# A decoder layer's final norm, moved from a closing pass over token blocks to lists of rows by expert group, worked on between the experts' steps

## Chip, core and metric

The kernel runs on one core of one Trainium2 chip. The core has five engines with a queue of instructions each: TensorE (PE in the rows, with its weight loads as PEld), VectorE (DVE), ScalarE (ACT), GpSimd (POOL), and SyncE (SP), which here only starts transfers. The metric is the device time of one execution in microseconds, lower is better.

## What is computed

The layer mixes 1024 tokens of width 1024 by two attention branches, adds the residual, and applies a first layer norm. Then comes a mixture of experts: each token picks one of 4 groups, and two of the 8 experts in that group. A second residual and layer norm give the output. The part that matters:

```python
grp = jnp.argmax(lg, axis=-1)                       # one group of 4 for each token
top_v, top_i = lax.top_k(lf, MOE_TOP_K)             # two experts of that group's 8
expert = grp[:, None] * EXP_PER_GROUP + top_i       # 0..31
...
    return (jax.nn.silu(g) * u) @ w_down[e]         # one expert on its tokens
...
h = layer_norm(ALPHA * h + ffn, ln2_g[l], ln2_b[l]) # over 1024 columns of each token
```

With the inputs of `setup_inputs()` the groups get 223, 248, 278 and 275 tokens, no expert gets more than 107, and 167 tokens of the last group use neither expert 30 nor expert 31.

## The kernel before

The program has three stages: projections and attention; the output projection with first norm and routing; and the experts, from about 1050 us to the end. The change is in the last.

**Experts.** The outer loop (L1676) goes over `seq`, 32 experts with 12 steps each. At a step PE multiplies one 128x1024 slab of weights with 128 gathered token rows: steps 0 to 7 are the gate and up weights, steps 8 to 11 the down weights. Everything is done in float32 split in two fp32r parts, so before a slab can be used ACT rounds it (`eh`, L1479) and DVE subtracts the rounded part from the raw slab (`el`, L1480). A step has six matmuls, four with `eh`, two with `el` (L1497). There are three `eh` buffers. `ahead` (L1657) emits the ACT and DVE work two to three steps ahead of the matmuls.

After step 7 comes a chain between engines: silu on ACT (L1504), product on DVE (`act`, L1505), transposes on PE (L1514), a rounding on ACT and a difference on DVE (`at`, L1516 and L1517). Then steps 8 to 11 run. `put` (L1519) scales the result on ACT (`y`) and adds its rows to `ybuf` in memory by an indirect transfer from POOL (L1523). `gather_rows` (L1372), also on POOL, fetches the rows of the expert after next from `hbuf`.

The order on PE, DVE, ACT and POOL is the order of the program text from here on (`manual_schedule`, L1668): each engine takes its instructions one after the other. SP's queue holds the weight loads (L1528). They go to a ring of 41 slots (`ring`, L1437) of 128x1024, and a load waits until the slot's last user is done.

**Final norm.** `ybuf` starts as the residual, and every expert adds into it. At (28,2), (28,4), (29,2) and (29,4) the marks `K` in `TAIL` (L65) spread the norm's gain and bias over partitions: two float32 matmuls (L1569) and a copy (L1570) each, in `final_gb`. After expert 30, `final_load` reads all eight blocks of 128 tokens. After the last step of expert 31 the long text in `TAIL` runs: `final_stats` and `final_stats_act` (L1577, L1583) take mean and variance of a block on DVE or ACT, `root` and `newton` (L1201, L1206) the inverse root, and gain and bias are applied on DVE, ACT and POOL (L1598 to L1613). Rows of expert 31 get its result from PSUM in `last_add` (L1625), are normed by `finish_rows` (L1540), and are written last by `put_rows` (L1549).

After that a hardware loop (L1713) makes extra passes for experts with over 128 tokens; its count `ntot` is 0 with these inputs.

Of the kernel before, what the change touches and what calls it, by code (L numbers as in the profile page):

```python
# [63 lines left out]
GBL = (22, 0)  # L64
TAIL = {(30, 11): "L0 L1 L2 L3 L4 L5 L6 L7", (28, 2): "K", (28, 4): "K", (29, 2): "K", (29, 4): "K", (31, 9): "P", (31, 11): "S0 V01 S1 N01 U0 A3 S2 V13 D2 G0p A5 S4 N13 V35 R D4 U1 B0p N35 G1p E2 H4 D5 B1p A7 Z A6 V58 U3 G3p D7 N58 E5 U6 G6p E7 B3d C6p F X"}  # L65
# [11 lines left out]
def tile_hybrid(ctx: ExitStack, tc: tile.TileContext, x, xT, w_t, w_gate, pos_k, w1_k, w2_k, pos_v, w1_v, w2_v,  # L77
# [1085 lines left out]
    nof, tok8 = (rc_pool.tile([128, NB], FP, name=n) for n in ("nof", "tok8"))  # L1163
    nid = rc_pool.tile([128, NB], I32, name="nid")
    nc.gpsimd.iota(tok8, pattern=[[128, NB]], base=0, channel_multiplier=1, allow_small_or_imprecise_dtypes=True)
# [120 lines left out]
    def out_route(b, L):  # L1286
# [8 lines left out]
        nc.vector.tensor_scalar(e4, e4, sc_[:, 1:2], None, op0=OP.is_equal)  # L1295
        nc.vector.tensor_scalar(e4, e4, -1.0, 1.0e30, op0=OP.add, op1=OP.mult)
# [21 lines left out]
        nc.vector.tensor_tensor(nof[:, b:b + 1], oh[:, 0, NE - 1:NE], oh[:, 1, NE - 1:NE], op=OP.add)  # L1318
# [94 lines left out]

    nc.vector.scalar_tensor_tensor(nid, nof, 4096.0, tok8, op0=OP.mult, op1=OP.add)
# [12 lines left out]
    nc.vector.tensor_copy(ntot, CX[:, 31:32])  # L1427
# [112 lines left out]
    def finish_rows(pl, z, o, g2, b2):  # L1540

        def centre(mean):
            nc.vector.scalar_tensor_tensor(o, z, mean, g2, op0=OP.subtract, op1=OP.mult)
        r, _, _ = stats(pl, z, EPS / ALPHA ** 2, centre, ((0, 512), (512, 1024)))
        for i in range(2):
            c = slice(i * 512, i * 512 + 512)
            nc.vector.scalar_tensor_tensor(o[:, c], o[:, c], r, b2[:, c], op0=OP.mult, op1=OP.add)
# [8 lines left out]
    zs = {}  # L1556

    def final_gb():

        kept.extend([next(er_at) for _ in range(3)])  # L1560
        gb, *ts = (p(n) for p, n in zip(kept, ("gb", "g2", "b2")))
        for i, src in enumerate((ln2_g, ln2_b)):
            nc.sync.dma_start(gb[32 * i:32 * i + 1, :], bass.AP(tensor=src.tensor, offset=src.offset,
                                                              ap=[[0, 1], [1, 1024]]))
        yield
        for i, t in enumerate(ts):
            for h in range(2):
                c, ps = slice(h * 512, h * 512 + 512), bank("pt")
                nc.tensor.matmul(ps, ones[32 * i:32 * i + 1, :], gb[32 * i:32 * i + 1, c], start=True, stop=True)  # L1569
                nc.scalar.copy(t[:, c], ps)  # L1570
                yield ts

    def final_load(b):
        zs[b] = er("zf")
        nc.sync.dma_start(zs[b], ybuf[b * 128:b * 128 + 128, :])

    def final_stats(b):  # L1577
        bs = fmt[:, b, 2:14].rearrange("p (a b) -> p a b", a=2)
        for i in range(2):
            nc.vector.bn_stats(bs[:, i], zs[b][:, i * 512:i * 512 + 512])  # L1580
        nc.vector.bn_aggr(fmt[:, b, 0:2], fmt[:, b, 2:14])

    def final_stats_act(b):  # L1583

        os_[b] = er("of")
        mean, var, s1 = fmt[:, b, 0:1], fmt[:, b, 1:2], fmt[:, b, 2:3]
        nc.scalar.activation(os_[b], zs[b], AF.Copy, scale=1.0 / D, accum_out=mean)
        nc.scalar.activation(os_[b], zs[b], AF.Square, scale=-1.0, bias=mean, accum_out=s1)
        nc.scalar.activation(var, s1, AF.Copy, scale=1.0 / D)

    def final_root(a, n):
        root(fmt[:, a:n], *(fmv[:, i, a:n] for i in range(3)), EPS / ALPHA ** 2)

    def final_newton(a, n):
        newton(fmt[:, a:n], *(fmv[:, i, a:n] for i in range(4)))

    def final_unit(b):
        nc.scalar.activation(zs[b], zs[b], AF.Identity, scale=fmv[:, 1, b:b + 1], bias=fmv[:, 3, b:b + 1])  # L1598

    def final_shift(b):  # L1600
        nc.vector.scalar_tensor_tensor(zs[b], zs[b], fmt[:, b, 0:1], gb[0], op0=OP.subtract, op1=OP.mult)

    def final_scale(b, skip=False):
        o = os_[b] if b in os_ else er("of")
        nc.vector.scalar_tensor_tensor(o, zs[b], fmv[:, 1, b:b + 1], gb[1], op0=OP.mult, op1=OP.add)
        final_put(b, o, skip)

    def final_gain(b, eng):
        eng.tensor_tensor(zs[b], zs[b], gb[0], op=OP.mult)

    def final_bias(b, eng, skip=False):
        o = os_[b] if b in os_ else er("of")
        eng.tensor_tensor(o, zs[b], gb[1], op=OP.add)  # L1613
        final_put(b, o, skip)

    def final_put(b, o, skip):
        if skip:
            outs.append(put_rows(o, nid[:, b:b + 1], outs + fulls))
        else:
            fulls.append(nc.sync.dma_start(out[0, b * 128:b * 128 + 128, :], o))  # L1620

    os_, outs, fulls, gb, hold = {}, [], [], [], [HOLD]
    fmt, fmv = e_pool.tile([128, NB, 14], FP, name="fmt"), e_pool.tile([128, 4, NB], FP, name="fmv")

    def last_add():  # L1625
        for i in range(2):
            c = slice(i * 512, i * 512 + 512)
            nc.vector.scalar_tensor_tensor(zl[:, c], last.dn[i], last.wgt, zg[:, c], op0=OP.mult, op1=OP.add)

    def final(text):  # L1630
        eng = {"p": nc.gpsimd, "d": nc.vector}
        f = {"L": final_load, "S": final_stats, "A": final_stats_act, "U": final_unit, "V": final_root, "N": final_newton,
             "D": final_shift, "E": final_scale, "H": lambda b: final_scale(b, True)}
        for t in text.split():
            if t[0] in "GBC":
                (final_gain if t[0] == "G" else final_bias)(int(t[1]), eng[t[2]], *[True][:t[0] == "C"])
            elif t == "W":
                hold[0] = 0
            elif t == "P":
                nc.scalar.preload_act_table_set(LNEXP)  # L1640
            elif t == "Z":
                last_add()
            elif t == "F":
                finish_rows(e_pool, zl, ol, *gb)
            elif t == "K":
                gb[:] = next(gb_)
            elif t == "R":
                rows_of(zg, last.ids)
            elif t == "X":
                outs.append(put_rows(ol, last.ids, outs))  # L1650
            else:
                f[t[0]](*map(int, t[1:]))
# [23 lines left out]
    for i, (e, k) in enumerate(seq):  # L1676
# [18 lines left out]
        if (e, k) in TAIL:  # L1695


            final(TAIL[e, k])
# [131 lines left out]
```

## Time and profile before

| | |
|---|---|
| median of 3 runs | 1719.45 us (1716.68 to 1721.52) |
| the profiled execution's own time | 1719.97 us |
| its span in the trace | 1718.2 us |
| busy, whole span: PE / DVE / ACT / POOL | 1587.5 / 1264.3 / 1103.8 / 439.2 us |
| transfers | 308.85 MB, mean 180 GB/s |

The span runs from the first instruction to the last event of the profiled execution; its own time is 1.8 us more. Times in rows are microseconds from the span's start unless marked ns. In a timeline row, "x7" merges seven instructions of one kind that ran without a pause, and a bracket tells how long the engine had been idle and whose end released it.

### The profile page before, as it was taken

The page shows a single profiled execution, that of the slowest core. Times are in us where ns is not written, and L with a number is a line of the kernel's source. Part 1 is how long each engine was busy: PE and PEld are TensorE (multiplying, and loading weights), DVE is VectorE, ACT ScalarE, POOL GpSimd, SP SyncE. Part 2 cuts the span into 40 slices and gives each one's busy share as a digit, 9 for nine tenths or more (in the row PEclk, how much of TensorE's full clock was granted, in tenths as well). Part 3 has the DMA queues.
Part 4 walks back from the last instruction along what each step waited for, and adds up shares of the span by engine and source line. Part 5 has one row for each costly group of instructions (what it writes and reads, how often), then busy time and mean ns, then how long its engine had stood idle before and what let it go on. Part 6 is the DMA issues. An engine that isn't in the chain of part 4 may idle for free. (4 is left out here: it accounts for less than half of the span.)

```text
span 1718.2 us, 24639 instructions
## 1 busy us (share of the span) xinstructions
PE 1587.5 (92%) x8114; PEld 1310.5 (76%) x8114; DVE 1264.3 (74%) x2680; ACT 1103.8 (64%) x2037; POOL 439.2 (26%) x390
## 2 busy tenths in 40 slices
PE   7999999998899999999799996999999999999970
PEld 6888888777678988788678895777777777777750
DVE  5555553347867774588877797998998899889786
ACT  4566665525557785578933014887887888788772
POOL 1011122341223332323610242221121212113134
PEclk9999999999999999999999997999999999999995
DMA  4111112232320111001356769999999999999532
GB/s 172 38 37 38 37 38 68 74 101 89 123 86 35 36 47 33 25 18 57 96 177 212 292 213 346 353 364 358 362 366 354 367 359 329 370 364 370 164 118 102
DMA packets 104518, 308.85 MB, mean 180 GB/s; under 512 B 20387, under 2 KB 24611, under 8 KB 104388
## 3 DMA queue, kind: packets, MB, share of 16 engines
q1 hardware_dynamic: 94228, 289.25, 46.0%
q0 software_dynamic: 10160, 18.00, 4.2%
q8 instruction: 65, 1.06, 0.3%
q14 instruction: 65, 0.53, 0.1%
HBM read 283.18 MB, written 41.17 MB: 189 GB/s over the span
## 5 line engine op out<-in xcount | busy, mean ns | idle before, releaser
L1480 DVE TENSOR_TENSOR el<-er,eh 128x1024 fp32r<-128x1024 f32 x384 | 448.1, 1219 | 31.7 <-ACT eh L1479 29.8
L1479 ACT CAST eh<-er 128x1024 fp32r<-128x1024 f32 x384 | 391.0, 1056 | 43.8 <-PE pt L1497 29.1
L232 PE MATMUL pp<-xh,wh 128*128 128x512 f32 x672 | 273.7, 407 | 1.6 <-DVE q L287 1.6
L234 PE MATMUL pp<-xh,wl 128*128 128x512 f32 x672 | 265.9, 396 | 0.0
L233 PE MATMUL pp<-xl,wh 128*128 128x512 f32 x672 | 264.4, 393 | 0.0
L1497 PE MATMUL av<-eh,xt 128*128 128x512 f32 x512 | 196.9, 395 | 1.4 <-ACT xt L1466 1.2
L1497 PE MATMUL pt<-eh,xt 128*128 128x512 f32 x512 | 196.2, 393 | 0.0
L1523 POOL DMA_INDIRECT ybuf<-y,idx x30 | 95.9, 3198 | 212.3 <-ACT y L1522 205.6
L234 PEld LDWEIGHTS pp<-xh,wl 128*128 128x128 f32 x672 | 127.1, 189 | 29.7
L232 PEld LDWEIGHTS pp<-xh,wh 128*128 128x128 f32 x672 | 127.5, 190 | 21.1 <-DVE q L287 2.0
L233 PEld LDWEIGHTS pp<-xl,wh 128*128 128x128 f32 x672 | 127.7, 190 | 19.4
L1497 PE MATMUL sc<-eh,at 128*128 128x512 f32 x512 | 141.4, 398 | 0.0
L892 POOL TENSOR_TENSOR pw<-pw,st 128x64 f32<-128x64 f32 (+5 forms) x128 | 85.9, 701 | 183.2 <-DVE st L887 156.5
L1497 PEld LDWEIGHTS av<-eh,xt 128*128 128x128 f32 x512 | 96.4, 188 | 27.8 <-ACT eh L1479 3.0
L1497 PEld LDWEIGHTS pt<-eh,xt 128*128 128x128 f32 x512 | 96.5, 189 | 22.2
L930 DVE TENSOR_TENSOR PT<-pt,PT 128x512 fp32r<-128x512 f32 (+1 forms) x136 | 90.9, 671 | 25.1 <-ACT PT L929 23.6
L1497 PEld LDWEIGHTS sc<-eh,at 128*128 128x128 f32 x512 | 93.6, 188 | 20.1 <-ACT eh L1479 0.4
L1497 PE MATMUL av<-el,xt 128*128 128x512 f32 x256 | 104.6, 409 | 0.0
L1497 PE MATMUL pt<-el,xt 128*128 128x512 f32 x256 | 100.9, 394 | 0.0
L1372 POOL DMA_INDIRECT xg<-hbuf,idx x31 | 33.3, 1075 | 253.3 <-PE pp L1460 239.6
L123 POOL TENSOR_TENSOR wl<-wr,wh 128x1024 fp32r<-128x1024 f32 x24 | 59.0, 2458 | 140.1 <-ACT wh L122 120.5
L929 ACT CAST PT<-pt 128x512 fp32r<-128x512 f32 (+1 forms) x136 | 76.7, 567 | 16.7 <-PE pt L922 15.0
(431 smaller groups left out, 3586.0 us busy)
## 6 DMA issues: line engine op xcount, KB each, us to landing
er<-in_w_gu_dram SPq DMA_DIRECT2D x256, 512.0 KB, 7.7
er<-in_w_dn_dram SPq DMA_DIRECT2D x128, 512.0 KB, 7.2
wr<-in_w_t_dram SPq DMA_DIRECT2D x44, 512.0 KB, 3.3
mgd<-mg SPq DMA_DIRECT2D x32, 256.0 KB, 2.0
G<-mgd SPq DMA_DIRECT2D x32, 256.0 KB, 3.4
xr<-in_xT_dram SPq DMA_DIRECT2D x8, 512.0 KB, 8.7
wo<-in_w_oT_dram SPq DMA_DIRECT2D x8, 512.0 KB, 4.8
wor<-in_w_out_dram SPq DMA_DIRECT2D x8, 512.0 KB, 7.6
```

Source lines behind the costliest of these rows:

```text
L123: (eng or nc.vector).tensor_tensor(lo, raw, hi.bitcast(FP), op=OP.subtract)
L232: nc.tensor.matmul(ps, wh[:, kk], xh[k][:, c], start=k == 0, stop=False)
L233: nc.tensor.matmul(ps, wh[:, kk], xl[k][:, c], start=False, stop=False)
L234: nc.tensor.matmul(ps, wl[:, kk], xh[k][:, c], start=False, stop=k == 7)
L892: nc.gpsimd.tensor_tensor(t, t, st[:, 1, hi_, i:i + 1].to_broadcast([128, w]), op=OP.mult)
L929: nc.scalar.copy(t[:, 0], src)
L930: nc.vector.tensor_tensor(t[:, 1], src, t[:, 0].bitcast(FP), op=OP.subtract)
L1372: nc.gpsimd.indirect_dma_start(out=t, out_offset=None, in_=hbuf, in_offset=bass.IndirectOffsetOnAxis(ap=ids, axis=0), bounds_check=S - 1, ...
L1479: nc.scalar.copy(wh, r)
L1480: nc.vector.tensor_tensor(wl, r, wh.bitcast(FP), op=OP.subtract)
L1497: nc.tensor.matmul(pss[h], a[j == 1][:, kk], (wl if j == 2 else wh)[:, h], start=o == 0 and j == 0, stop=o == n - 1 and j == 2)
L1523: nc.gpsimd.indirect_dma_start(out=ybuf, out_offset=bass.IndirectOffsetOnAxis(ap=self.ids, axis=0), in_=y, in_offset=None, bounds_check=S ...
```

## The change

- While the second expert runs, a generator `lists` builds a table of token numbers sorted by group. Tokens that use expert 30 or 31 are left out of the last group's list. This takes 31 small DVE instructions, three small matmuls, eight indirect transfers from POOL to a table `tabf` in memory, and one load of it on SP. Gain and bias are loaded already spread over partitions; the four `K` marks are gone.
- `FIN` names eleven blocks of up to 128 rows of a list and the step (expert, k) where each begins: nine between experts 10 and 28, two in expert 31. A twelfth block holds expert 30's rows, a thirteenth expert 31's.
- A block's work is spread over steps by `at(i, f)`, run at the end of step i: `take` (an indirect gather of `ybuf` rows on POOL, four steps ahead), `fin_mean` and `fin_square` on ACT in the next two steps, `turn` in the third (two integer instructions on DVE give a first guess of the inverse root, three rounds of four 128x1 instructions on POOL refine it, and DVE subtracts the mean and multiplies by the gain), and `end` in the fifth (DVE multiplies by the root and adds the bias, POOL scatters the rows to the output). Rows go in place, in a slot `zf` of the ring; `fm` is a 128x8 tile of statistics, `any` a scratch output.
- Expert 30's block adds that expert's result from PSUM at (30,11) and is normed during expert 31. Expert 31's block is normed after the last matmul, as before, but with nothing ahead of it.
- The extra passes' count is raised to 32 if a list overflows its blocks (`NFB`).

```diff
-GBL = (22, 0)
-TAIL = {(30, 11): "L0 L1 L2 L3 L4 L5 L6 L7", (28, 2): "K", (28, 4): "K", (29, 2): "K", (29, 4): "K", (31, 9): "P", (31, 11): "S0 V01 S1 N01 U0 A3 S2 V13 D2 G0p A5 S4 N13 V35 R D4 U1 B0p N35 G1p E2 H4 D5 B1p A7 Z A6 V58 U3 G3p D7 N58 E5 U6 G6p E7 B3d C6p F X"}
+NFB = 3, 3, 3, 2
+FIN = {(10, 0): (0, 0), (12, 0): (0, 1), (14, 0): (0, 2), (18, 0): (1, 0), (20, 0): (1, 1), (22, 0): (1, 2),
+       (25, 0): (2, 0), (26, 0): (2, 1), (28, 0): (2, 2), (31, 0): (3, 0), (31, 1): (3, 1)}
...
+    def lists():
+        kept.extend([next(er_at) for _ in range(3)])
+        gb[:] = (p(n) for p, n in zip(kept, ("g2", "b2", "any")))
+        for t, src in zip(gb, (ln2_g, ln2_b)):
+            nc.sync.dma_start(t, bass.AP(tensor=src.tensor, offset=src.offset, ap=[[0, 128], [1, 1024]]))
...
+        for b in range(NB):
+            s_ = nc.gpsimd.indirect_dma_start(out=tabf, out_offset=bass.IndirectOffsetOnAxis(ap=at[:, b:b + 1], axis=0),
+                                              in_=nid[:, b, :], in_offset=None, bounds_check=128 * 32 - 1,
+                                              oob_is_err=False)
...
+    def fin_mean(z, f):
+        nc.scalar.activation(gb[2], z, AF.Copy, scale=1.0 / D, accum_out=f[:, 0:1])
+
+    def fin_square(z, f):
+        nc.scalar.activation(gb[2], z, AF.Square, scale=-1.0, bias=f[:, 0:1], accum_out=f[:, 1:2])
+        nc.vector.tensor_scalar(f[:, 2:3], f[:, 1:2], VE, None, op0=OP.add)
+
+    def fin_root(f, act=False):
...
+            b = t.bitcast(I32)
+            nc.vector.tensor_scalar(b, v.bitcast(I32), 1, None, op0=OP.logical_shift_right)
+            nc.vector.tensor_scalar(r.bitcast(I32), b, -1.0, float(0x5f3759df), op0=OP.mult, op1=OP.add)
+            for _ in range(3):
+                nc.gpsimd.tensor_tensor(t, r, r, op=OP.mult)
+                nc.gpsimd.tensor_tensor(t, t, v, op=OP.mult)
+                nc.gpsimd.tensor_scalar(t, t, -0.5, 1.5, op0=OP.mult, op1=OP.add)
+                nc.gpsimd.tensor_tensor(r, r, t, op=OP.mult)
...
+    def fin_shift(o, z, f):
+        nc.vector.scalar_tensor_tensor(o, z, f[:, 0:1], gb[0], op0=OP.subtract, op1=OP.mult)
+
+    def fin_scale(o, f, cut=1):
...
+            nc.vector.scalar_tensor_tensor(o[:, c], o[:, c], f[:, 3:4], gb[1][:, c], op0=OP.mult, op1=OP.add)
...
+    def block(i, ids, x=None):
+
+        b = {}
+
+        def take():
+            b["z"], b["f"] = er("zf"), fin_new()
+            rows_of(b["z"], ids)
+
+        def add():
             for h in range(2):
+                add_rows(b["z"], b["z"], x, h)
+
+        def turn():
+            for _ in fin_root(b["f"]):
+                pass
+            fin_shift(b["z"], b["z"], b["f"])
+
+        def end():
+            fin_scale(b["z"], b["f"])
+            s_ = put_rows(b["z"], ids, outs)
...
+        at(i - 4 if x is None else i - 3, take)
+        if x:
+            at(i, add)
+            i += 4
+        at(i + 1, lambda: fin_mean(b["z"], b["f"]))
+        at(i + 2, lambda: fin_square(b["z"], b["f"]))
+        at(i + 3, turn)
+        at(i + 5, end)
...
+    block(12 * NE - 13, idx[:, NE - 2, 0:1], ex[NE - 2])
+    for (e, k), (c, i) in FIN.items():
+        block(12 * e + k, idf[:, 8 * c + i, 0:1])
...
+        zl, ol = er("zl"), er("ol")
+        finish_rows(ol, zl, last, zg)
+        put_rows(ol, last.ids, outs)
+    at(12 * NE - 5, lambda: rows_of(zg, last.ids))
+    at(12 * NE - 4, lambda: nc.scalar.preload_act_table_set(LNEXP))
+    at(12 * NE - 1, final)
```

How the queues change at three places (each row is an instruction in an engine's order, "x8" eight alike; line numbers of the changed kernel are one higher here for the same line).

DVE, steps 0 to 7 of an expert, before:

```order
L1467 TENSOR_TENSOR xt<-pp,xt 128x512
L1480 TENSOR_TENSOR el<-er,eh 128x1024
L1467 TENSOR_TENSOR xt<-pp,xt 128x512
L1480 TENSOR_TENSOR el<-er,eh 128x1024 x8
L1505 TENSOR_TENSOR act<-act,av 128x256
L1505 TENSOR_TENSOR act<-act,pt 128x256
```

and in expert 10 of the changed kernel, the first with a block:

```order
L1468 TENSOR_TENSOR xt<-pp,xt 128x512
L1481 TENSOR_TENSOR el<-er,eh 128x1024 x5
L1625 TENSOR_SCALAR fm<-fm 128x1
L1481 TENSOR_TENSOR el<-er,eh 128x1024
L1639 TENSOR_SCALAR fm<-fm 128x1
L1640 TENSOR_SCALAR fm<-fm 128x1
L1650 SCALAR_TENSOR_TENSOR zf<-zf,fm,g_11025 128x1024
L1481 TENSOR_TENSOR el<-er,eh 128x1024 x2
L1655 SCALAR_TENSOR_TENSOR zf<-zf,fm,b_11026 128x1024
L1506 TENSOR_TENSOR act<-act,av 128x256
L1506 TENSOR_TENSOR act<-act,pt 128x256
```

Five instructions of the block now stand among the eight `el` of the steps, the last of them straight ahead of the silu chain's `act`.

ACT at the same place, before:

```order
L1479 CAST eh<-er 128x1024 x2
L1521 ACTIVATE y<-sc,idx 128x512
L1522 ACTIVATE y<-sc,idx 128x512
L1479 CAST eh<-er 128x1024 x6
L1504 ACTIVATE act<-av 128x256
```

and in expert 10 of the changed kernel:

```order
L1522 ACTIVATE y<-sc,idx 128x512
L1523 ACTIVATE y<-sc,idx 128x512
L1480 CAST eh<-er 128x1024 x2
L1621 ACTIVATE any,fm<-zf 128x1024
L1480 CAST eh<-er 128x1024
L1624 ACTIVATE any,fm<-zf,fm 128x1024
L1480 CAST eh<-er 128x1024 x3
L1505 ACTIVATE act<-av 128x256
```

The two passes over the block stand between the casts for steps 4 and 5, and 5 and 6.

POOL at the end of the program (`xg` is the buffer into which expert 31's rows of `ybuf` are gathered for the final add), before:

```order
L1372 DMA xg_9419<-hbuf,idx 128x1024
L1523 DMA ybuf<-y,idx 1024x1024 x2
L1609 TENSOR_TENSOR zf<-zf,g_15003 128x1024
L1536 DMA xg_9419<-ybuf,idx 128x1024
L1613 TENSOR_TENSOR of<-zf,b_15004 128x1024
```

and in the changed kernel, the end of the third and last root refinement in expert 31 and what follows:

```order
L1642 TENSOR_TENSOR fm<-fm 128x1
L1643 TENSOR_TENSOR fm<-fm 128x1
L1644 TENSOR_SCALAR fm<-fm 128x1
L1645 TENSOR_TENSOR fm<-fm 128x1
L1607 DMA out_dram<-zf,idf 1024x1024
L1537 DMA xg_9421<-ybuf,idx 128x1024
L1607 DMA out_dram<-zf,idx 1024x1024
L1607 DMA out_dram<-ol,idx 1024x1024
```

The gather for the last add now stands behind 36 refinement instructions and two scatters of the blocks in expert 31.

## Rows read from the trace of the kernel before

**Rows 1.** Busy time in one stretch of the experts: PE, PEld, DVE, ACT, POOL, clock, DMA share, GB/s.

```profile
1200.00:1300.00 100.00, 98.47 (x450) 77.30 (x449) 88.14 (x97) 82.42 (x109) 18.47 (x11) 1.00 0.99 364
```

**Rows 2.** Who waited for whom, 1100 to 1600 us: total us, times, longest us.

```profile
PEld av L1497 <- DVE el L1480: 9.3, 26, 0.4
...
ACT eh L1479 <- DMA er<-in_w_gu_dram: 5.6, 17, 0.3
```

**Rows 3.** The same for SP's queue, 960 to 1640 us.

```profile
SPq L1528 <- PE pt L1497: 219.7, 229, 3.1
```

**Rows 4.** Timeline of one expert, ACT and DVE, steps 1 to 7 and the chain's start.

```profile
1321.25 8.05 DVE L1480 TENSOR_TENSOR el<-er,eh 128x1024 fp32r<-128x1024 f32 x7
...
1325.61 1.05 ACT L1479 CAST eh<-er 128x1024 fp32r<-128x1024 f32 x1 [0.34 <-PE pt L1497]
...
1331.36 0.42 DVE L1505 TENSOR_TENSOR act<-act,av 128x256 f32<-128x256 f32 x1 [0.67 <-ACT act L1504]
```

**Rows 5.** POOL's timeline: scatters of two neighbouring experts, then of experts 27 and 28.

```profile
1303.77 2.45 POOL L1523 DMA_INDIRECT ybuf<-y,idx  x1 [6.75 <-ACT y L1522]
1322.62 2.44 POOL L1523 DMA_INDIRECT ybuf<-y,idx  x1 [6.76 <-ACT y L1522]
...
1586.17 2.44 POOL L1523 DMA_INDIRECT ybuf<-y,idx  x1 [6.75 <-ACT y L1522]
1607.52 2.44 POOL L1523 DMA_INDIRECT ybuf<-y,idx  x1 [6.76 <-ACT y L1522]
```

**Rows 6.** Timeline of the end: last matmuls, last add, last block's statistics, last scatter.

```profile
core 0 of [0], span 1718.2 us
...
1663.47 0.62 PE L1497 MATMUL sc<-el,at 128*128 128x512 f32 x2
...
1683.56 1.39 DVE L1628 SCALAR_TENSOR_TENSOR zl<-sc,idx,xg 128x512 f32<-128x512 f32 x2
...
1698.58 1.27 DVE L1190 BATCH_NORM_STATS2 bs<-zl 128x6 f32<-128x512 f32 x2
...
1703.65 0.98 POOL L1550 DMA_INDIRECT out_dram<-ol,idx  x1 [4.14 <-DVEq L1713]
```

**Rows 7.** Timeline of the end: instructions of the kinds that a block is made of.

```profile
1668.26 1.04 ACT L1587 ACTIVATE of<-zf 128x1024 f32<-128x1024 f32 x1
...
1669.42 1.15 ACT L1588 ACTIVATE of<-zf,fmt 128x1024 f32<-128x1024 f32 x1
...
...
1670.72 1.27 DVE L1601 SCALAR_TENSOR_TENSOR zf<-zf,fmt,g 128x1024 f32<-128x1024 f32 x1
...
1677.10 0.16 DVE L1208 TENSOR_TENSOR fmv<-fmv 128x2 f32<-128x2 f32 x1
1677.30 0.16 DVE L1209 SCALAR_TENSOR_TENSOR fmv<-fmv 128x2 f32<-128x2 f32 x1
```

**Rows 8.** Timeline of the end: POOL and DVE arithmetic at the same time.

```profile
1672.97 2.34 POOL L1613 TENSOR_TENSOR of<-zf,b 128x1024 f32<-128x1024 f32 x1
1673.35 1.98 DVE L1208 TENSOR_TENSOR fmv<-fmv 128x2 f32<-128x2 f32 x1
...
1688.63 5.65 POOL L1609 TENSOR_TENSOR zf<-zf,g 128x1024 f32<-128x1024 f32 x2 [1.72 <-ACT zf L1598]
1688.71 6.65 DVE L1605 SCALAR_TENSOR_TENSOR of<-zf,fmv,b 128x1024 f32<-128x1024 f32 x2
```

**Rows 9.** POOL's instructions by shape: busy us, mean ns of one, idle us before them.

```profile
L892 POOL TENSOR_TENSOR pw<-pw,st 128x640 f32<-128x640 f32 x32 | 41.3, 1292 | 0.0
...
L892 POOL TENSOR_TENSOR pw<-pw,st 128x64 f32<-128x64 f32 x64 | 25.4, 396 | 183.2 <-DVE st L887 156.5 <-ACT PT L929 17.9 <-PE sc L371 7.8
...
L892 POOL TENSOR_TENSOR pw<-pw,st 128x128 f32<-128x128 f32 x8 | 3.2, 401 | 0.0
```

**Rows 10.** Transfers, from issue to landing (last figure, us), and POOL issuing a scatter.

```profile
xg<-ybuf,idx POOLq DMA_INDIRECT x1, 5.1
...
1682.71 1.83 POOL L1550 DMA_INDIRECT out_dram<-of,nid  x1 [2.69 <-DVE of L1605]
```

More of the change, by code (lines that the diff above doesn't have):

```diff
@@ L1538, in rows_of @@
                                      bounds_check=S - 1, oob_is_err=False)
[L1540 to L1547, printed above, removed]
+    outs, gb = [], []
@@ L1573, in final_load @@
[L1573 to L1606, printed above, removed]
@@ L1623, in tile_hybrid @@
[L1623 to L1652, printed above, removed]
@@ new lines, in fin_shift, with finish_rows @@
+    def fin_shift(o, z, f):
+        nc.vector.scalar_tensor_tensor(o, z, f[:, 0:1], gb[0], op0=OP.subtract, op1=OP.mult)
+    def fin_scale(o, f, cut=1):
+        for i in range(cut):
+            c = slice(i * 1024 // cut, (i + 1) * 1024 // cut)
+            nc.vector.scalar_tensor_tensor(o[:, c], o[:, c], f[:, 3:4], gb[1][:, c], op0=OP.mult, op1=OP.add)
+    def finish_rows(o, z, x=None, g=None):
+        f = fin_new()
+        bs = e_pool.tile([128, 2, 6], FP, name="bs", tag="bs", bufs=2)
+        mt = e_pool.tile([128, 2], FP, name="mt", tag="mt", bufs=2)
+        for i in range(2):
+            if x:
+                add_rows(z, g, x, i)
+            nc.vector.bn_stats(bs[:, i], z[:, i * 512:i * 512 + 512])
+        nc.vector.bn_aggr(mt, bs.rearrange("p a b -> p (a b)"))
+        nc.vector.tensor_scalar(f[:, 2:3], mt[:, 1:2], float(D), VE, op0=OP.mult, op1=OP.add)
+        r = fin_root(f, x is not None)
+        next(r)
+        fin_shift(o, z, mt)
+        next(r)
+        fin_scale(o, f, 2)
@@ new lines, in tile_hybrid, with final @@
+    steps_ = lists()
+    for i in (13, 16, 17, 18, 19):
+        at(i, lambda: next(steps_, None))
+    block(12 * NE - 13, idx[:, NE - 2, 0:1], ex[NE - 2])
+    for (e, k), (c, i) in FIN.items():
+        block(12 * e + k, idf[:, 8 * c + i, 0:1])
+    last, zl = ex[NE - 1], None
+    def final():
+        nonlocal zl
+        zl, ol = er("zl"), er("ol")
[3 more added lines that the diff above has]
+    at(12 * NE - 4, lambda: nc.scalar.preload_act_table_set(LNEXP))
@@ L1691, in tile_hybrid @@
             ex[e].put()
-        if (e, k) == GBL:
-            gb_ = final_gb()
-            next(gb_)
-        if (e, k) in TAIL:
-            final(TAIL[e, k])
-        if (e, k) == (NE - 2, 11):
-            zl, ol = er("zl"), er("ol")
+        for f in hooks.pop(i, ()):
+            f()
+    assert not hooks
     mo_.close()
```

134 lines of the change are left out of this document (96 added, 38 removed).

## Prediction

> **What bounds the kernel now.** I read the windows first, to see which engine fills the experts' stage. In 100 us of it PE is busy 98.5, DVE 88.1 and ACT 82.4 us, and POOL 18.5 [rows 1]. So PE sets the pace, at 18.85 us an expert, the distance of two scatters [rows 5], and DVE is left 11.9% of that, 2.2 us.
>
> Then the waits: does PE ever wait, and for whom? It does, 26 times in 500 us and always about 0.35 us, for DVE's difference `el` [rows 2]. That is once per expert for that kind of wait, so DVE has no lead over PE at that point. The transfers are no limit: ACT waited 5.6 us in all for weights [rows 2], while SP waited 219.7 us for PE to free a slot [rows 3], so the loads run as far ahead as the ring lets them.
>
> Then the timeline of one expert, for where DVE and ACT have their idle time. DVE runs seven `el` in 8.05 us without a pause, 1.15 us each. ACT pauses 0.34 us, for PE, before the cast of step 6. DVE's one larger pause is 0.67 us, at the head of the silu chain [rows 4]. What is put on DVE before that point delays the chain, with 0.67 us to absorb it.
>
> Last, the end. The last matmuls end at 1663.47 + 0.62 = 1664.1 us, the span at 1718.2 [rows 6]: 54.1 us with PE idle.
>
> **What the change removes.** After the last matmul there remain two adds (1.4 us, as the row of 1683.56), what now lies between the last block's statistics and its scatter (1703.65 - 1698.58 = 5.1), and what lies from there to the end (1718.2 - 1703.65 = 14.5) [rows 6]: 21.0 us where there were 54.1. **Saved: 33.1 us.** The `K` marks made expert 28 take 1607.52 - 1586.17 = 21.35 us in place of 18.85 [rows 5], and expert 29 has two as well. **Saved: 2 x 2.5 = 5.0 us.** The eight reads of `ybuf` and six of the eight writes of the output leave SP's queue after the last weight load, where nothing waits behind them.
>
> **What a block costs.** I take expert 10, with the queues as the two places on DVE and ACT show them.
> 1. *ACT.* The mean takes 1.16 us from its start to the next start, the square, by its 1.15 and the same 0.12 for reading the sum, 1.27 [rows 7]. Both stand before the cast of step 6, which had 0.34 us to spare, so it comes 2.1 us late. DVE ran some 0.3 us behind that cast (the sixth `el` of the merged row starts at 1321.25 + 5 x 1.15 = 1327.0, the cast ends at 1326.7 [rows 4]), so its `el` of step 6 is 1.8 us late.
> 2. *DVE's own work.* The instruction on the variance falls into that wait. Two small ones are 0.2 us each from start to start, shift and scale 1.27 us each [rows 7]: 2.9 us.
> 3. *The refinement on POOL.* Twelve dependent 128x1 instructions, and the scale on DVE waits for the last. No row has this shape. From 128x640 to 128x128 the time falls by 1.74 ns a column, which leaves 0.18 us at one column; 128x64 took 0.40 [rows 9]. I take 0.20, as nearer the line, and 0.05 between two: 3.0 us if POOL is left alone.
> It is not: a 128x2 instruction that is 0.16 us elsewhere [rows 7] took 1.98 us on DVE beside one on POOL, and ended when that did [rows 8]. And two POOL and two DVE instructions took turns, POOL's pair 5.65 us where 2 x 2.34 is its own, DVE's 6.65 where 2.5 is [rows 8]. So each waits while the other runs. Between the guess and the scale DVE has three long instructions (shift, `el` of steps 7 and 8). Each lets one refinement step through at its end: three steps, 0.6 us more for DVE. The other nine, 9 x 0.25 = 2.25, run while DVE waits at the scale. Together 2.85 us.
> 4. *Absorbed:* the 0.67 us ahead of the chain.
>
> Behind the waiting scale stands `act`, for which PE's transposes and steps 8 to 11 wait, so all of it reaches PE: 1.8 + 2.9 + 2.85 - 0.7 = 6.9 us. **Nine blocks: 62 us.**
>
> Whether that [rows 8] also holds for `el` against such tiny instructions, no row shows. The Trainium skill's page "SBUF — State Buffer", section "Who interferes with whom", says that a DVE instruction with two SBUF inputs contends with a GpSimd instruction that reads SBUF, and that whichever starts first holds the shared ports for its whole length. `el`, shift and scale are of that kind, so by the page point 3 costs what I took; without it, nothing.
>
> **Expert 31** has three blocks. The first costs 6.9 us. The second's refinement queues on POOL behind the first's: between the two scales DVE has two small instructions (0.4), the third block's shift (1.27), the lock (0.6), nine refinement steps (2.25) and the second scale (1.27), 5.8 us. The two adds of expert 30's result take 1.4. Sum 14 us. The third refinement comes after, beside steps 8 to 11. But the gather for the last add stands behind it, as the POOL place shows: after the second scale POOL issues a scatter (1.83 us), runs twelve steps (3.0, plus three waits of 1.2 for `el`), issues the next scatter (1.83), then the gather, which lands 5.1 us after issue [rows 10]: 15.3 us. PE needs some 8.7 from there to its end (an estimate: four steps at 18.85 / 12, and 2.4 for the chain). So the add waits some 6 us. **20 us.**
>
> **The lists.** 31 small dependent DVE instructions at 0.2 us, less the 0.67: **5.5 us.** The three matmuls and one ACT pass lie beside them. Eight indirect transfers hold POOL some 10 us in expert 1; the next gather is needed 18.85 us later. SP waits for the table before one weight load; the ring of 41 slots, which the loads keep filled [rows 3], covers that with some three experts' steps. If it didn't, PE would wait a few us once.
>
> **Sum:** -33.1 - 5.0 + 5.5 + 62 + 20 = +49.4. Against the profiled execution's own 1719.97 us that is 1769.4; that execution is 0.5 us above the median, so **1769 us**. With a refinement step of 0.40 + 0.05 us, point 3 is 5.25, nine blocks cost 22 us more and expert 31 some 6: 1797, the upper end.
>
> **Rivals.**
> - *No lock for small steps.* The refinement runs beside DVE's 3.5 us of shift and two `el`, and costs nothing. A block is 1.8 + 2.9 - 0.7 = 4.0 us. Nine are 36, expert 31 is 4.0 + 2.9 + 1.4 and 3 for the gather, 11. Sum -38.1 + 5.5 + 47 = +14: 1734 us. For it: no row shows so short an instruction on POOL. Against it: the short one on DVE waited [rows 8].
> - *The idle time takes the blocks* (the other side). DVE's 2.2 us an expert absorb most of a block's 3.1 us (three small instructions, shift, scale), ACT's 17.6% all of its 2.4, and refinement hides. Then 0.9 us a block, 8 for nine, 4 for expert 31: -38.1 + 5.5 + 12 = -21, 1699 us. It decides where a block costs under some 2.8 us: (38.1 - 5.5 - 7) / 9. Against it: most of that idle time lies inside the silu chain, after the block's last instruction, and 0.67 is left before it [rows 4].
> - *Memory is the limit.* The transfers' share is 0.99 at 364 GB/s [rows 1]. Then DVE's and ACT's work would hide, and the rows' way through memory, 4.2 MB read and 4.2 written, would cost 8.4 MB / 364 GB/s = 23 us: -38.1 + 23 = -15, 1704 us. Against it: SP waits for PE, not PE for loads [rows 2, 3]. The Trainium skill's page "SBUF — State Buffer", section "SBUF: two separate sides", puts HBM to one core at about 358 GB/s and calls HBM almost always the bottleneck; the trace's rate agrees, its waits don't.
> - *The change doesn't do what it says:* a list overflows and 32 extra passes run. The group sizes (223, 248, 278 of 384; 167 of 256) exclude it.
>
> **How the numbers follow.** About 0.3% (5 us) is what a measurement can tell from no change. The forecast, lock and late gather, has 0.62. The rival without lock has 0.23, the idle time 0.07, memory 0.02. A block of just under 3 us, so no change, has 0.04, and over the upper end is 0.02. Faster is 0.07 + 0.02 = 0.09, same 0.04, slower 0.87. The range runs from 1730, which takes in the rival without lock, to 1797; it leaves out 0.15. The forecast's own range is 1750 to 1797.
>
> **What would show it.** Expert 10 takes about 25.7 us between scatters and expert 11 18.85. On DVE the scale of expert 10 stands behind an idle stretch of 2 us or more that POOL's refinement ended, and POOL's first steps last over 1 us, the later ones 0.2. ACT's cast of step 6 no longer waits for PE. In expert 31 the add on DVE waits for a transfer. From the first add to the end it is 21 us. An expert with a block at under 21.6 us would prove me wrong on the sign; one at 22.8, with the scale not waiting, on the lock.

## The result and the profile after

| | before | changed |
|---|---|---|
| median | 1719.76 us (1716.68 to 1721.52, 4 runs) | 1766.64 us (1762.49 to 1769.04, 4 runs) |
| ratio, 95% interval | 1 | 1.0272 (1.0244 to 1.030) |
| span of the profiled execution | 1718.2 us | 1767.2 us |
| mean granted clock | 0.972 | 0.963 |

The kernel became 2.7% slower, 47 us. 1769 was forecast.

The rows that answer to those shown of before, first the busy time in a stretch with one block, in expert 10 (columns as in [rows 1]):

```profile
1200.00:1300.00 100.00, 93.81 (x412) 73.09 (x411) 84.32 (x94) 77.12 (x102) 27.04 (x24) 0.97 0.95 344
```

PE is busy 93.8 of 100 us in place of 98.5, and POOL's 27.0 is no sign of a limit. Who waited for whom, 1100 to 1640 us (total, times, longest):

```profile
PEld av L1515 <- DVE act L1506: 31.1, 8, 3.9
...
PEld av L1498 <- DVE el L1481: 24.1, 35, 1.8
DVE zf L1655 <- POOL fm L1645: 20.3, 8, 2.5
```

The first and the third are new: PE's transposes wait for `act`, and DVE's scale waits for POOL's refinement, 2.5 us a block. This is the wait that the forecast put at the head of the silu chain. The second was 9.3 us in 26 waits of 0.4 at most [rows 2]; now single ones are 1.8.

I measure experts by PE's first transpose of the chain (L1515), since the scatters of [rows 5] shift by some 3 us where they wait for a block's gather. PE's rows for experts 9, 10 (with a block) and 11:

```profile
1244.15 0.41 PE L1515 MATMUL av<-ident,act 128*128 128x128 f32 x2
...
1269.21 0.69 PE L1515 MATMUL av<-ident,act 128*128 128x128 f32 x2 [3.66 <-DVE act L1506]
...
1289.88 0.40 PE L1515 MATMUL av<-ident,act 128*128 128x128 f32 x2
```

Expert 10 takes 25.06 us and expert 11 takes 20.67, where an expert without a block takes 18.82 by the same mark. So the block costs 6.24 us up to its chain and 1.85 more behind it. Over the 20 intervals from expert 9 to expert 29 it is 1683.69 - 1244.15 = 439.54 us, less 20 x 18.82 = 376.4: **63.1 us for nine blocks**, 55.3 of them ahead of the chains and 7.8 in the experts behind. The blocks are not alike: up to the chain experts 14 and 22 cost 5.62 and 5.63 us, expert 10 costs 6.24, and expert 26, which follows a block directly, 7.25.

Now the timeline of DVE in expert 10, from the `el` of step 5 to the chain, then POOL's:

```profile
1257.98 1.23 DVE L1481 TENSOR_TENSOR el<-er,eh 128x1024 fp32r<-128x1024 f32 x1 [0.98 <-ACT eh L1480]
...
1260.06 1.22 DVE L1481 TENSOR_TENSOR el<-er,eh 128x1024 fp32r<-128x1024 f32 x1 [0.78 <-ACT eh L1480]
1261.20 0.15 DVE L1639 TENSOR_SCALAR fm<-fm 128x1 int32<-128x1 int32 x1
1261.38 0.15 DVE L1640 TENSOR_SCALAR fm<-fm 128x1 int32<-128x1 int32 x1
1261.45 1.27 DVE L1650 SCALAR_TENSOR_TENSOR zf<-zf,fm,g 128x1024 f32<-128x1024 f32 x1
1262.64 2.35 DVE L1481 TENSOR_TENSOR el<-er,eh 128x1024 fp32r<-128x1024 f32 x2
1267.54 1.28 DVE L1655 SCALAR_TENSOR_TENSOR zf<-zf,fm,b 128x1024 f32<-128x1024 f32 x1 [2.54 <-POOL fm L1645]
1268.74 0.41 DVE L1506 TENSOR_TENSOR act<-act,av 128x256 f32<-128x256 f32 x1
```

```profile
1261.63 1.15 POOL L1642 TENSOR_TENSOR fm<-fm 128x1 f32<-128x1 f32 x1 [3.14 <-DVE fm L1640]
1262.86 1.05 POOL L1643 TENSOR_TENSOR fm<-fm 128x1 f32<-128x1 f32 x1
1264.00 1.04 POOL L1644 TENSOR_SCALAR fm<-fm 128x1 f32<-128x1 f32 x1
1265.13 0.19 POOL L1645 TENSOR_TENSOR fm<-fm 128x1 f32<-128x1 f32 x1
...
1267.31 0.19 POOL L1645 TENSOR_TENSOR fm<-fm 128x1 f32<-128x1 f32 x1
```

All parts of the price stand here in one column of starts. DVE waits 0.98 + 0.78 = 1.76 us for casts that ACT does late. Not all of that is the price of ACT's two passes, since in expert 10 the mean itself waits for its rows. In expert 14 it doesn't, the first of the two waits is 0.37 us, and the sum is 1.15. ACT's row of expert 10, then DVE's of expert 14:

```profile
1255.86 1.06 ACT L1621 ACTIVATE any<-zf 128x1024 f32<-128x1024 f32 x1 [0.50 <-DMA zf<-ybuf,idf]
...
1348.15 1.23 DVE L1481 TENSOR_TENSOR el<-er,eh 128x1024 fp32r<-128x1024 f32 x1 [0.37 <-ACT eh L1480]
```

Guess, shift and scale take 0.25 + 1.19 + 1.20 = 2.64, with the variance instruction 2.8. Three refinement steps last over a microsecond, each ending just after one of DVE's three long instructions; the nine others take 0.19 with 0.08 between, and DVE stands 2.54 us until they are done. `act` comes last, with PE behind it.

And the end: PE's last matmuls, the add, its gather and the last scatter.

```profile
1742.27 0.63 PE L1498 MATMUL sc<-el,at 128*128 128x512 f32 x2
```

```profile
1747.33 0.75 DVE L1676 SCALAR_TENSOR_TENSOR zl<-sc,idx,xg 128x512 f32<-128x512 f32 x1 [5.49 <-DMA xg<-ybuf,idx]
```

```profile
1743.04 1.04 POOL L1537 DMA_INDIRECT xg<-ybuf,idx  x1 [0.30 <-PEq L1784]
...
1754.00 0.97 POOL L1607 DMA_INDIRECT out_dram<-ol,idx  x1 [8.61 <-DVEq L1784]
```

From the first add to the end it is 1767.2 - 1747.3 = 19.9 us, and the add waited 5.5 us for a gather that POOL issued at 1743.04, after PE had ended. Before, from the last add to the end it was 34.6 us [rows 6].

What I had not looked for is the clock. Busy time and clock in three pieces around expert 10's chain:

```profile
1262.00:1268.00 6.00, 2.17 (x11) 1.27 (x9) 3.46 (x4) 0.77 (x2) 4.59 (x12) 1.00 0.95 332
1268.20:1274.80 6.60, 5.59 (x17) 4.69 (x18) 5.22 (x8) 4.17 (x6) 2.14 (x2) 0.50 0.51 190
1275.00:1281.00 6.00, 6.00 (x28) 4.86 (x27) 4.92 (x6) 5.40 (x7) 0.43 (x1) 1.00 0.85 277
```

PE had work for 2.2 of 6 us, and then the granted clock is 0.50 for 6.6 us, the level of 1.2 GHz, just when steps 8 to 11 run. Four matmuls take 2.05 us there and 1.08 at full clock:

```profile
1270.83 2.05 PE L1498 MATMUL sc<-eh,at 128*128 128x512 f32 x4
...
1275.58 1.08 PE L1498 MATMUL sc<-eh,at 128*128 128x512 f32 x4
```

Each of the nine blocks has such a stretch, of 3.4 or 6.8 us; before, the experts had none, up to the end of PE's work. This is the time behind the chains: 1.85 us in expert 11, behind a stretch of 6.8 us, and 0.73 to 1.00 in the seven experts behind a stretch of 3.4.

### The profile page after: what moved, and what is told of

Read it like the earlier page. It is cut to its first block, busy times and chain, and to the rows that moved or that the text cites. A ratio compares the mean times of both kernels' runs of the same rounds, so it can differ in the third digit from the quotient of the medians.

```text
span 1767.2 us, 24910 instructions
## 1 busy us (share of the span) xinstructions
PE 1608.2 (91%) x8109; PEld 1326.8 (75%) x8109; DVE 1270.3 (72%) x2730; ACT 1111.4 (63%) x2050; POOL 489.5 (28%) x562
## 5 line engine op out<-in xcount | busy, mean ns | idle before, releaser
L1498 PE MATMUL sc<-eh,at 128*128 128x512 f32 x512 | 154.2, 426 | 0.0
L1524 POOL DMA_INDIRECT ybuf<-y,idx x30 | 68.9, 2295 | 206.1 <-ACT y L1523 145.9
L1498 PEld LDWEIGHTS sc<-eh,at 128*128 128x128 f32 x512 | 102.6, 206 | 22.8 <-ACT at L1517 0.4
```

The source lines that it names most:

```text
L1498: nc.tensor.matmul(pss[h], a[j == 1][:, kk], (wl if j == 2 else wh)[:, h], start=o == 0 and j == 0, stop=o == n - 1 and j == 2)
L1524: nc.gpsimd.indirect_dma_start(out=ybuf, out_offset=bass.IndirectOffsetOnAxis(ap=self.ids, axis=0), in_=y, in_offset=None, bounds_check=S ...
```

## The experiments

All times are medians beside runs of the kernel before on the same chip; "after" is the changed kernel. The price of the nine blocks is taken from each trace as above, from the last expert ahead of them to the last one behind, less 18.82 an expert; it leaves out the time before the experts, by which the traces differ by up to 8.5 us (expert 0's transposes start between 1062.2 and 1070.7).

**Scale moved behind the chain.**

```diff
-        at(i + 5, end)
+        at(i + (8 if i < 12 * NE - 12 else 5), end)
```

> Of the nine blocks in experts 10 to 28, only the scale (and its scatter) moves, from the end of step 5 to the end of step 8, behind the silu chain; POOL's twelve refinement steps stay. Theory (the price is the time DVE stands at the scale with act behind it): the chain is late by ACT's 1.76 us, the guess 0.25 and the shift 1.19, less 0.67, so 2.5 us, and the scale costs 0 to 1.2 us more behind the chain. Nine blocks cost 22 to 33 us in place of 63: 1726 to 1737 us, 8 more if the clock still falls after each block. POOL's steps last about 1.1 us beside el and 0.19 us where DVE pauses, and el stays at 1.15 us. Rival (a POOL step delays DVE as much as DVE delays it): twelve steps beside el and the chain cost DVE some 0.2 us each, 2.4 us a block, and the gain is given back: 1750 to 1758 us, with el pairs longer than 2.35 us.

Measured: 1757.0 us, ratio 1.0229 (1.0186 to 1.0271). The time is that of the rival, the trace is not: a pair of `el` still takes 2.35 us with POOL's steps beside it, and expert 10 costs 21.05 + 20.02 - 37.64 = 3.4 us, as the theory has it. But the nine cost 53 us, because another wait, 2.1 us in all in the changed kernel, has grown:

```profile
ACT any L1621 <- DMA zf<-ybuf,idf: 21.5, 8, 5.8
```

With the ninth block, which that window leaves out, it is 25.3 us. ACT's mean stands for rows that have not landed, and the casts stand behind it. POOL's steps were 1.05 us beside `el` and 0.19 beside `act`, so the lock is one of DVE against POOL, and not the other way. The number alone would have confirmed the wrong theory.

**Refinement left out.** `rounds=0` for the nine blocks in place of 3.

> The three rounds of refinement are left out of the nine blocks in experts 10 to 28 (those rows get the first guess of the root); all else stays in its place. Theory: a block costs ACT's 1.76 us, DVE's own 2.76 us, less 0.67: 3.85 us, nine are 35 in place of 63: 1738 us, 8 more if the clock still falls. Rival (the wait at the scale lies beside something else that ends as late): 1766 us. If it comes out within 5 us of the kernel with the late scale, POOL's steps beside DVE cost DVE nothing.

Measured: 1736.2 us, ratio 1.0090 (1.0058 to 1.0122), the theory's number. Nine blocks 38.6 us, with 13.3 us of ACT's waits for rows in it, where the changed kernel has 2.1. So I compare experts 14 and 22, where neither kernel's mean waits: 3.00 and 3.09 us up to the chain in place of 5.62 and 5.63. The refinement is worth 2.6 us a block there, and what is left is less than the theory's 3.85, which held the 0.6 us that expert 10 waited on account of its rows.

This run also bears on the time behind the chains. PE waits only 1.0 us at `act`, the granted clock stays at 1.0 behind every chain, and the expert behind takes 18.5 to 18.6 us in place of 19.6 to 20.7.

The time is not within 5 us of the late scale's, as the expectation wanted for POOL's steps to cost DVE nothing, since the late scale's rows came late. The kernel at 1738.1 us below, where most of them come in time, is within 2 us.

**Refinement on DVE.**

```diff
-                nc.gpsimd.tensor_tensor(t, r, r, op=OP.mult)
+                eng.tensor_tensor(t, r, r, op=OP.mult)
```

and so on for all four, `eng=nc.vector` in the nine blocks.

> In the nine blocks of experts 10 to 28 the twelve refinement steps run on DVE, between the guess and the shift. Theory (the price of the refinement is its serial length ahead of act, not POOL): twelve steps of 0.19 us are 2.3 us on DVE in place of 2.54 us of waiting, so a block costs the same within 0.3 us: 1762 to 1768 us. Rival (the shared lock between POOL and DVE is the price, and away from it the steps cost little): 2 us less a block, 1745 to 1750 us.

Measured: 1760.3 us, ratio 1.0249 (1.0218 to 1.0280), and 58.2 us for the nine. Twelve steps went at 0.19 us from start to start, 2.3 us, and DVE no longer waited at the scale. It is 0.5 us a block less, a little more than the theory allowed, and far from the rival's 2 us. But the means waited 7.2 us for rows here. In expert 22, where they waited in neither kernel, the block costs 5.37 us up to its chain in place of 5.63, as the theory has it, and the expert behind takes 18.58 us in place of 19.72, which the theory did not expect. PE's wait of 3.7 us now stands at `el` of step 7, and the half clock begins 3.0 us ahead of the chain. So what is paid up to the chain is twelve dependent steps ahead of `act`, on whichever engine.

**ACT's passes into ACT's pause.** Mean and square at step 6 of the two experts before, ahead of the silu. First try:

```diff
-        at(i - 4 if x is None else i - 3, take)
...
-        at(i + 1, lambda: fin_mean(b["z"], b["f"]))
-        at(i + 2, lambda: fin_square(b["z"], b["f"]))
+        at(i - 22 if early else i - 4 if x is None else i - 3, take)
...
+        at(i - 18 if early else i + 1, lambda: fin_mean(b["z"], b["f"]))
+        at(i - 6 if early else i + 2, lambda: fin_square(b["z"], b["f"]))
```

> In the nine blocks the gather comes 18 steps earlier, the mean is taken at step 6 of the expert two before and the square at step 6 of the expert before, each in ACT's 1.50 us pause ahead of the silu; guess, refinement, shift and scale stay at steps 3 and 5. The three blocks of experts 25, 26 and 28 move to 26, 28 and 30, and the rows stand in two slots of their own. Theory (ACT's two passes ahead of the casts of steps 5 and 6 make DVE 1.76 us late, and a pass in the pause costs nothing): 9 x 1.76 = 16 us less, 1751 us; DVE no longer waits 0.78 and 0.98 us for casts in these experts. Rival (DVE would have been late anyway, since it stands at the scale until POOL is done): POOL's refinement then starts earlier by the same amount and nothing is lost there, so this rival wants 1764 to 1768 us, with a longer wait at the scale. Second rival (a pass of 1.27 us in the pause delays the silu): 1767 us or more, with the chain of the expert before late.

Measured: 1825.4 us, ratio 1.0608 (1.0578 to 1.0638): worse than the theory and the first rival, and with the late chain of the second, but not by the pass. Two rows tell why, POOL's and ACT's:

```profile
1226.44 1.05 POOL L1537 DMA_INDIRECT zf<-ybuf,idf  x1 [7.77 <-DMA ybuf<-y,idx]
```

```profile
1233.81 1.06 ACT L1621 ACTIVATE any<-zf 128x1024 f32<-128x1024 f32 x1 [10.77 <-DMA zf<-ybuf,idf]
```

At step 2 the last expert's scatter into `ybuf` has just been issued; the gather must wait for its landing, and the mean, four steps later, stood 10.8 us in front of the silu. It tested the gather's place and not the pause. Second try, with the gather at `i - 28`, step 8 of the expert three before:

> Again mean and square at step 6 of the two experts before the block, in ACT's 1.50 us pause ahead of the silu, but with the gather at step 8 of the expert three before, so that the rows have landed (in the first try the gather was issued at step 2, waited 7.8 us for the last scatter's landing, and ACT stood 10.8 us at the mean). Nine blocks at experts 11, 13, 15, 19, 21, 23, 27, 29 and 30; guess, refinement, shift and scale stay at steps 3 and 5. Theory: ACT's 1.76 us are saved in each block, 16 us, 1751 us, 1745 if the clock falls less often; the casts of steps 5 and 6 come on time. Rival (POOL's wait takes it back, or the pass delays the silu): 1762 us or more, with a wait at the scale over 4 us or a chain that starts late in the experts before.

Measured: 1756.1 us, ratio 1.0211 (1.0183 to 1.0240). In eight of the nine the expert with the block now takes 23.05 to 23.40 us up to its chain, 4.2 to 4.6 over 18.82, where it was 5.6 to 7.3. The least are 1.4 us apart (4.23 and 5.62): that is what the passes cost, not the theory's 1.76. Experts with a pass alone take 18.81 to 18.89, so a pass in the pause costs nothing. Nine blocks still cost 50.5 us (none is behind the last, in expert 30), 12.6 less in place of 16, and the time lies between theory and rival: the expert behind is up to 2.05 us late again, as PE still stands at `act` and the half clock follows.

**Earlier gather, with the late scale.**

```diff
-        at(i - 4 if x is None else i - 3, take)
+        at(i - 8 if i < 12 * NE - 13 else i - 4 if x is None else i - 3, take)
```

> The kernel with the late scale, and in the nine blocks the gather of the rows also comes four steps earlier (at step 4 of the expert before, in place of step 8). Theory (there the late scale paid as forecast, 3.4 us in expert 10, but ACT's mean then waited 21.5 us in eight blocks for gathers that POOL issued late, behind a scatter's landing): the waits go, nine blocks cost 30 to 33 us, and it is 1733 to 1738 us. Rival (the transfers have no room left, so the rows land late whenever they are asked for): the mean, or the casts, still wait, 1750 to 1757 us.

Measured: 1753.0 us, ratio 1.0210 (1.0178 to 1.0242), nine blocks 43.8 us: the rival's number again, and again not its reason. Blocks without a wait cost 3.0 us (20.64 + 20.02 - 37.64), others up to 7.4, with 16.5 us of waits at the mean in five. POOL's rows between two blocks:

```profile
1271.37 1.03 POOL L1607 DMA_INDIRECT out_dram<-zf,idf  x1 [2.79 <-DVE zf L1655]
1273.52 8.19 POOL L1524 DMA_INDIRECT ybuf<-y,idx  x1 [1.11 <-ACT y L1523]
1289.71 1.16 POOL L1537 DMA_INDIRECT zf<-ybuf,idf  x1 [8.00 <-DMA ybuf<-y,idx]
```

The gather waits for the scatter that follows the block's own scatter to the output. So I moved that one:

**Output scatter behind the expert's own.**

```diff
             fin_scale(b["z"], b["f"])
+            if i < 12 * NE - 13:
+                at(i + 17, out_)
+            else:
+                out_()
+
+        def out_():
             s_ = put_rows(b["z"], ids, outs)
```

> The kernel with late scale and early gather, and the nine blocks' scatters to the output come at step 5 of the next expert, behind the expert's own scatter and the next block's gather, in place of right ahead of that scatter. Theory (there, the output scatter stood 1.1 us ahead of the expert's scatter, which then held POOL 8.2 us where it is 1.6 to 2.5 us elsewhere; the next block's gather came late and ACT's mean waited 16.5 us in five blocks): the long scatters and the waits go, a block costs 3.0 to 3.5 us, 1735 to 1741 us. Rival (the transfers of a block have no room in memory's time, wherever they stand): the mean waits as before, 1750 to 1756 us.

Measured: 1738.1 us, ratio 1.0113 (1.0091 to 1.0136), nine blocks 31.9 us, 3.5 each. The waits at the mean fell from 16.5 to 4.7 us. Half of my reason was wrong: the expert's scatter still holds POOL 8.2 us. But it lands earlier, and the gather behind it is issued 13.6 us after it in place of 16.2:

```profile
1272.51 8.19 POOL L1524 DMA_INDIRECT ybuf<-y,idx  x1 [4.93 <-ACT y L1523]
1286.10 1.48 POOL L1537 DMA_INDIRECT zf<-ybuf,idf  x1 [5.39 <-DMA ybuf<-y,idx]
```

The same bytes move as in the changed kernel, in 28 us less: memory was not the limit.

**The last add's gather earlier** (step 4 of expert 31 in place of 7).

```diff
-    at(12 * NE - 5, lambda: rows_of(zg, last.ids))
+    at(12 * NE - 8, lambda: rows_of(zg, last.ids))
```

> In expert 31 the gather for the last add is issued at step 4, ahead of the third block's refinement and of both output scatters on POOL, in place of step 7; nothing else changes. Theory (the add waited 5.5 us for this gather alone, since POOL issued it late): the add waits for PE, and the end comes 5 to 5.5 us earlier, 1761 us, less up to 1 us by which the first output scatter is later. Rival (PE's end in expert 31, at half clock, is nearly as late as the landing was): 1764 to 1767 us.

Measured: 1765.3 us, ratio 1.0266 (1.0250 to 1.0282), the rival's number. The add no longer waits for the gather. It follows the third scale, which comes 1.4 us later, and PE ends at about the same time. From the last transposes to the end it is 28.8 us in place of 33.0. That 4.2 us did not show in the medians, so it ran again beside the changed kernel, five runs each:

> The changed kernel itself once more, for the comparison with the one below on the same chip: ratio 1.0272 to the kernel before, as measured, 1766 us.

> The kernel with the earlier gather for the last add once more, with more rounds. In its first profile the stretch from the last transposes to the end was 28.8 us, against 33.0 in the changed kernel, while the nine blocks had cost 2.5 us more than there, and the two medians differed by 1.3 us. Theory (the end is 4.2 us shorter, the rest is chance): 4 us less than the kernel above, ratio lower by 0.0025. Rival (the earlier gather costs in the experts what it saves at the end): within 1 us of the kernel above.

Measured: the changed kernel 1770.6 us, ratio 1.0306 (1.0283 to 1.0329), and with the earlier gather 1766.2, ratio 1.0277 (1.0256 to 1.0299). The difference of 4.4 us is the one expected, but the intervals overlap. In both traces of the edited kernel the nine blocks also cost some 3 us more (65.6 and 66.3 us, against 63.1 and 63.2), which is what the rival said; in expert 9 a scatter holds POOL 7.0 us in place of 2.4 and the block's gather is late. So the 4.2 us at the end are shown; what the edit is worth to the whole kernel is not settled.

**A version with every piece in a pause.** Each half of shift and scale (128x512) has its own place: one at step 6 ahead of `act`, one between `at` and the next `el`.

```diff
+        for e, f in (shift, b.shift), (scale, b.scale):
+            at(12 * e + 6, lambda f=f: f(0))
+            pauses[e] = lambda f=f: f(1)
...
+            pauses.pop(e, lambda: None)()
```

> A version built from what the runs say: every piece of a block lies in a pause. Gather at step 8 (one at step 4) with a full expert to land, mean and square in ACT's pause ahead of the silu of two experts (one mean at step 1), refinement on POOL behind the square, shift and scale cut in two halves of 512 columns, one in DVE's 0.66 us pause ahead of act, one in its 0.53 us pause behind at. Seven blocks in place of nine (two suffice for groups of 223 and 248), the lists' small instructions spread over experts 1 to 6, the table loaded from POOL's queue, the last add's gather ahead of the refinements of expert 31, expert 30's and the last group's rows partly behind the last norm. Theory: lists 2 us, a block 1 to 2 us, expert 31 and the end 29 us less than before, K marks 5 less: 1695 to 1705 us, faster than before. Rival (memory becomes the limit once the blocks hide: seven blocks move 7.3 MB at 364 GB/s, 20 us): 1712 to 1720 us, with ACT waiting for weights.

Measured: 1710.3 us, ratio 0.9959 (0.9939 to 0.9979), faster than before, but behind its theory and 2 us from the rival's range. The rival's mark is missing, as ACT waited 0.3 us in all for weights between 1100 and 1640 us. Most experts with a piece took 18.7 to 18.9 us. What was lost stood in a few places: the table's eight scatters held POOL so long that PE waited for an expert's rows (4.5 us, with half clock behind it), two means waited 6.6 us together, and in expert 31 a variance instruction on DVE waited 6.9 us for ACT with the last add behind it. These were mended:

> The version with every piece in a pause, with what its profile showed amiss mended: eight scatters of the table in two groups of four (they held up one gather, 6 us in experts 6 and 7); the mean of expert 25 two steps later and one gather four steps earlier (waits of 2.9 and 3.7 us, 5.7 us in all); in expert 31 the gathers ahead of the refinement on POOL, the variance step of expert 30's rows no longer ahead of other work on DVE (a wait of 6.9 us), and the last two roots by ACT's table in place of POOL, whose steps held the last scatter 6 us. Theory: 20 to 24 us less, 1686 to 1692 us. Rival (the pauses are now full and the waits only move): 1698 us or more.

Measured: **1694.0 us, ratio 0.9860 (0.9838 to 0.9882)**, 24.5 us less than before and 73 less than the changed kernel. It is 2 us above the theory's upper end, well short of the rival's 1698. The stretch of [rows 1] in it, and DVE around the chain of an expert with a piece:

```profile
1200.00:1300.00 100.00, 98.51 (x451) 77.31 (x451) 90.45 (x104) 84.77 (x114) 28.98 (x27) 1.00 0.99 366
```

```profile
1274.38 1.23 DVE L1483 TENSOR_TENSOR el<-er,eh 128x1024 fp32r<-128x1024 f32 x1 [0.15 <-ACT eh L1482]
1275.52 0.74 DVE L1664 SCALAR_TENSOR_TENSOR zf<-zf,fm,g 128x512 f32<-128x512 f32 x1
1276.27 0.42 DVE L1508 TENSOR_TENSOR act<-act,av 128x256 f32<-128x256 f32 x1
...
1278.31 0.42 DVE L1520 TENSOR_TENSOR at<-pt,at 128x256 fp32r<-128x256 f32 x1 [0.27 <-ACT at L1519]
1278.65 0.74 DVE L1664 SCALAR_TENSOR_TENSOR zf<-zf,fm,g 128x512 f32<-128x512 f32 x1
```

PE is busy 98.5 us again, at full clock, with DVE at 90.5 in place of 88.1. From expert 8 to expert 30 it takes 416.25 us, 2.2 over 22 x 18.82, for seven blocks. (Groups of 223 and 248 rows need two blocks; the changed kernel gave them three.) The lists cost 1.1 us here.

## Why the prediction was right, point by point

The time, the direction and the main mechanism (the chain waits for the block's scale, and that for POOL's refinement behind the lock) were right. That the time came out within 3 us is partly luck, as two terms were off in opposite directions. Below, each term of the sum with what it measured.

- **End, -33.1:** from the last transposes to the end it was 1718.2 - 1656.8 = 61.4 us, and is 33.0 with the late gather in it. That is -28.4, or some -33 with the 4.2 to 5.5 us of the gather taken out.
- **K marks, -5.0:** experts 28 and 29 took 21.34 and 21.35 by the transposes, 5.05 over two plain ones. Right.
- **Lists, +5.5:** 6.2 (23.17 and 20.69 us in experts 1 and 2). Not as the text has it: the 31 instructions made expert 1 4.35 us late, under the 5.5, and the rest, in expert 2, follows a stretch at half clock.
- **Nine blocks, +62:** 63.1, but not for the reasons given alone. Up to the chain a block cost 55.3 / 9 = 6.1 us, where the text had 6.9. ACT's 1.8 was 1.15 in experts 14 and 22 (mean and square take 1.05 and 1.14 us from start to start in expert 10, not 1.16 and 1.27). In the others it was 1.4 to 2.1, in four of them with a wait for the block's rows of up to 0.68 us, which no term held. DVE's own 2.9 was 2.8. POOL's 2.85 was 2.54 by the wait and 2.6 by leaving it out. The step that failed is "each waits while the other runs", as far as it made three POOL steps cost DVE 0.6 us: shift and two `el` take 3.54 us from start to end, and 3.55 in the run with nothing on POOL beside them. Behind the chain came what no term held: 7.8 us in all of slowed matmuls, since PE's wait of 3.7 us was followed by half clock. "Expert 11 18.85" was therefore wrong, by 1.8. Too much ahead of the chain, nothing behind it: the two errors nearly cancel, and that is luck.
- **Expert 31, +20:** 12.8 us up to its transposes where the text had 14, and 5.5 of waiting for the gather where it had 6.

Sum by the trace: -28.4 - 5.05 + 6.2 + 63.1 + 12.8 = 48.7, with 0.14 us of a later start close to the 49.0 by which the spans differ; forecast 49.4.

The choice that mattered was 0.20 + 0.05 us for a refinement step, off the line through 128x640 and 128x128 and not the 0.40 of [rows 9]: 0.19 + 0.08. And that the lock of [rows 8] holds for such tiny instructions: 1.05 to 1.15 us beside `el` or shift, 0.19 beside nothing, beside small instructions, and beside `act`. The Trainium skill's page "SBUF — State Buffer", section "Who interferes with whom", agrees on both sides: `el` and shift have two inputs in SBUF, `act` has one in PSUM. Its rule that whichever is first holds the ports shows in the blocks only for DVE: POOL's steps of 0.19 us cost it no visible time, while [rows 8] has DVE waiting for a long one of POOL.

The rivals: without the lock twelve steps of 0.27 us would have ended before the second `el` did, the wait would be 0, and 1734 would have been near; the wait of 2.5 us in each block refutes it. The idle time did not take the blocks because of where they stood, and the last version shows that it can: DVE and ACT have the room, in pauses of 0.5 to 1.5 us. Memory, at 1704 us, is refuted by the run at 1694, which reads and writes every row too, and by the trace: ACT's casts waited 5.6 us in all for weights before and not once in the changed kernel (1100 to 1640 us).

Of the signs named, these came: the scale's wait, POOL's long and short steps, casts that no longer wait for PE, the add that waits for a transfer, and 19.9 us behind it for 21. Expert 11 at 18.85 did not.

## To carry to other kernels

An engine's idle share alone does not tell what it can take on; the pauses do, by length and by what stands behind them. Work that is cut to fit a pause (half a shift of 0.74 us at a pause of 0.66) left experts at 18.7 to 18.9 us. The same work ahead of the instruction that PE waits for cost its length but for the 0.67 us of that pause, every dependent small step included, and PE's slower clock on top. A wait read from one block need not hold for the next: 0.6 of expert 10's 1.76 us came from rows that landed late. When an experiment's time matches one theory, look in its trace for that theory's mark before believing it: twice here the time was the rival's and the cause was a gather that waited for a scatter.

## What the runs showed of the hardware

- In the changed kernel PE waited some 3.7 us at `act` in each block, and within 2 us of the end of each such wait the granted clock fell to 0.5, for 3.4 or 6.8 us. So it did at each wait of 3.7 us at `el` in the run with refinement on DVE. At a wait of 3.1 us in expert 1 it fell in the first of these two kernels and not in the second. In the last version, where no wait of PE in the experts was over 1.2 us, it stayed at 1.0 through all of them.
- A 128x1 instruction on POOL takes 0.19 us, 0.27 from start to start; on DVE it is 0.15 to 0.16, and 0.19 from start to start.
- The issue of an accumulating scatter holds POOL mostly for 1.6 to 2.5 us, but for 7.0 in five of the 31 scatters of the kernel before, and for 8.2 in eight of 31 in each kernel with the late scale and once in the last version. A few took 3 to 5. Which scatters are long is not explained; moving another scatter away did not shorten them.
